# Values and six projection units of the second token half moved ahead of the attention loop

## The chip, the cores and the metric

The kernel runs on one core of a Trainium2 chip. The metric is the time of one execution on the device, in microseconds (us). Five engines matter here: PE (TensorE, matmuls), DVE (VectorE), ACT (ScalarE), POOL (GpSimd) and SP (SyncE), whose in-order queue issues nearly all DMA transfers.

## The reference

One layer of an encoder over 2048 tokens of 1024 features in float32, with 16 heads of 64:

```python
h = rmsnorm(x, norm_0)
q, k, v, gate = split(h @ w_in_0, 4)              # each 2048 x 1024
# tokens form a grid of 32 rows x 64 columns; a query sees 8 rows x 16 columns of keys
s = q . k / 8 + rpb[head, row offset, column offset]   # outside the window: -1e30
o = softmax(s) . v
x = x + (o * silu(gate)) @ w_out_0
out = rmsnorm(x, norm_f)
```

## The kernel before

All large matmuls are made of float32 values split in a high and a low part (`hi`, `lo`, or `h`, `l`): three products (hi.hi, hi.lo, lo.hi) replace one. A weight or input block is split by one ACT copy and one DVE or POOL subtraction.

The instruction order of every engine is written by hand (`manual_schedule`): each engine and the SP queue run their lists in program order, and wait by semaphores. `store(key, lag, f)` puts an action off until `lag` more filler matmuls have been issued.

Tokens are handled in four quarters `c` (0 to 3) of 512 tokens, and eight head pairs `p`. The kernel has two parts.

`stage_one` (L413) projects tokens 0 to 1023 (c = 0, 1): first the values (`values_of`, L468, matmul L475), then twelve units, one for each of `k`, `q`, `g` (gate) and four weight column groups `j`. A unit is computed with seven block products in place of eight (`product`, L508, matmul L517): 7 x 12 = 84 matmuls of 128x512, against 96 in the plain form. The price is sums of weight blocks on DVE (`sum_`, L502), sums of results (`add`, `out_`) and a scaling on POOL (L535). `give` (L341) splits q and k into high and low and stores them to DRAM (`q_hi`, `q_lo`, `k_hi`, `k_lo`).

Then a loop over 64 pieces (`pairs`; a piece is one head pair, one block `T` of 8 token rows, two of four column blocks `C`) does the attention. For each piece: `scores` (L819: 12 matmuls L832, then a fused add-and-minimum L839 on DVE and an exponential L842 on ACT), `normalise` (L845: reciprocal on DVE, scaling L850 on POOL), `turns` (L862: transposes L855 on PE, copies out of PSUM L879 on ACT and L880 on DVE) and `values` (L886, matmuls L900). Scores of piece i stand between the transposes and the values of piece i-1. Loads of a piece come from DRAM: `load_v` (L778, eight transfers `vt` of 36 to 64 KB for one piece, at L789), `load_qk` (L760, `kt` twice and `qt` twice for two pieces), `load_sg`, `load_e` (the bias table of a head pair, from which `bias`, L806, makes the masked tables `em`).

Between the pieces `feed` (L1114) issues filler matmuls: first `projections` (L715), the remaining plain projections of tokens 1024 to 2047 (c = 2, 3; `group` L365 with matmuls L374 to L378, `group_v` L384 with L393 to L397), then `outputs` (L1050), the output projection (L1087 to L1091). The list `amount` sets how many filler matmuls a piece gets, about 27 for most:

```python
amount = [44.0] * 2 + [(8 * 192 - 48 - 30 - 88) / 50] * 50 + [29.0] * 5 + [46.0] * 4 + [48.0] * (N + 1 - 61)
```

Pieces come in the order: block T = 0 of all head pairs, then T = 1, 2, 3 of head pair 0, of head pair 1, and so on. At most eight transfers of the SP queue are under way: each takes one of eight completion semaphores in turn, and waits for the transfer eight before it.

Of the kernel before, what the change touches and what calls it, by code (L numbers as in the profile page):

```python
# [25 lines left out]
EPS = 1e-6  # L26
# [44 lines left out]
def build(ctx, tc, x, xr, xt, wg, rpb, w_out, n0, nf, masks, out):  # L71
# [3 lines left out]
    q_hi = [dram.tile([128, S], F32, name=f"q_hi{p}") for p in range(NP)]  # L75
    q_lo = [dram.tile([128, S], F32, name=f"q_lo{p}") for p in range(NP)]
# [12 lines left out]
    wp = pool("wp", 10)  # L89
# [5 lines left out]
    xp = pool("xp", 4)  # L95
# [63 lines left out]
    def use_item(it):  # L159
# [3 lines left out]
        if kind == "x":  # L163
            split_x(a, b, t)
        elif kind == "w":
# [13 lines left out]
            (nc.gpsimd if (b + u) % 2 and state["half"] > 1 else nc.vector).tensor_tensor(l, t, h.bitcast(F32), OP.subtract)  # L179
# [8 lines left out]
    def square(t, half, tile_):  # L188
        c = t // 4
        if c not in rows:  # L190
            rows[c] = tiny.tile([128, 8], F32, name="ss")
        i = t % 4 if half is None else 2 * (t % 4) + half
        nc.scalar.activation(tile_, tile_, AF.Square, accum_out=rows[c][:, i:i + 1])

    def stats(c):
        ss = rows.pop(c)
        m = tiny.tile([128, 8], F32, name="m")[:, :4]
        if c < 2:
            nc.vector.tensor_tensor(m, ss[:, 0:8:2], ss[:, 1:8:2], OP.add)
            ss = m  # L200
        nc.vector.tensor_scalar(m, ss[:, :4], 1.0 / D, EPS, op0=OP.mult, op1=OP.add)
        rsqrt(rt[:, 4 * c:4 * c + 4], m, 4)
# [38 lines left out]
    for n, (k, j, ph, c) in enumerate(halves):  # L241
        a = (KINDS[k] + j, ph)
        wi = [("w", (u, ph), b) for b in range(4) for u in units(k, j)] if a not in seen else []
        xi = [("x", b, c) for b in range(NK)] if c not in seen else []
# [8 lines left out]
    def may_use(it):  # L253
        kind, a, b = it
        d = state["done_halves"]
        if kind == "w":
# [3 lines left out]
            return sum(1 + (KINDS["v"] <= t[0] < KINDS["g"]) for t in live | {tiles_(a, b)}) <= 10  # L260
# [80 lines left out]
    def give(kind, hp, c, tmp):  # L341
# [3 lines left out]
        if kind == "g":  # L345
# [38 lines left out]
    def group_v(w, t):  # L384
        c, o = divmod(t, 4)
        o = slice(o * 128, o * 128 + 128)
        p = bank(512, "pv")
        for k in range(NK):
            need(("x", k, c))
            for u in range(2):  # L390
                need(("w", (w[0] + u, w[1]), k // 2))
            h, l = wh[w, k // 2][:, k % 2], wl[w, k // 2][:, k % 2]
            nc.tensor.matmul(p, hh[k, c][:, o], h, start=(k == 0), stop=False)  # L393
            yield 1
            nc.tensor.matmul(p, hh[k, c][:, o], l, start=False, stop=False)  # L395
            yield 1
            nc.tensor.matmul(p, hl[k, c][:, o], h, start=False, stop=(k == NK - 1))  # L397
            if k % 2 and t % 4 == 3 and state["half"] == last_use["w", w]:
                freed.add((*w, k // 2))
            yield 1  # L400
            if k in (2, 5):
                consume(1)
        evac_v((w[0] - KINDS["v"]) // 2, t, p)

# [8 lines left out]
    def stage_one():  # L413
        us = [(k, j) for j in range(4) for k in "kqg"]
        order7 = (1, 6, 2, 7, 5, 4, 3)
        seq = [(n, P) for n in range(len(us)) for P in order7]
        uses = {1: ("A11", "B11"), 2: ("A12", "B21"), 3: ("S4", "B22"), 4: ("A22", "T4"),
                5: ("S1", "T1"), 6: ("S2", "T2"), 7: ("S3", "T3")}
        quarter = {"A11": 0, "A12": 1, "A21": 2, "A22": 3}
        A, F, B, U, W = {}, {}, {}, {}, {}  # L420
        X1 = {f: [(xs([128, 512], F32R, "h"), xs([128, 512], F32R, "l")) for _ in range(4)]
              for f in ("B12", "B11", "B21", "B22")}
        spot = mkp([128, 3, 512], F32, "spot")
        land = {f: [p([128, n], F32, "land")[:, :512] for _ in range(4)]
                for f, p, n in (("x12", kp, 960), ("x22", qp, 512), ("x11", vp, 512))}
        land["x21"] = [spot[:, k] for k in range(3)] + [lp([128, 512], F32, "land")]
        slots = [(mp, 512)] * 6 + [(vp, 512)] * 2 + [(sp, 512)] * 2 + [(pa, 768)] * 2 + [(vp, 512)] * 4
# [146 lines left out]
        for k in range(4):  # L574
            load_x("x12", k)
# [655 lines left out]
```

## Time and profile before

| | |
|---|---|
| median of 3 runs | 1109.18 us (1106.75 to 1109.65) |
| the profiled execution | 1107.81 us |
| its span, first to last instruction | 1105.7 us |
| mean granted TensorE clock | 0.995 |
| PE busy | 1086.1 us (98%) |
| DVE, ACT, POOL busy | 691.2, 512.7, 368.7 us |
| first score matmul, last value matmul | about 350 us, about 1032 us |
| moved by DMA | 228.32 MB, mean 206 GB/s |

A busy share is the time in which an engine had an instruction under way. Matmuls overlap in the pipeline, so the mean duration of one (about 390 ns for 128x512) is longer than the distance between two. The DMA share is the mean over the core's 16 DMA engines. "x" before a number counts instructions; an arrow `<-` in a wait names what the engine waited for.

### The profile page before, as it was taken

Reading aid. Unit: us, or ns where it says so; the run is one execution under the profiler, and the core shown is the slowest. Engines: PE = TensorE matmul, PEld = TensorE weight load, DVE = VectorE, ACT = ScalarE, POOL = GpSimd, SP = SyncE. Lnnn points to the kernel's source line nnn. Section 1 sums busy time; section 2 is a strip of 40 time slices with the busy share of each in tenths; the row PEclk is TensorE's granted clock in tenths of the full one; section 3 lists DMA queues with packets and bytes.
Section 4 is the critical chain, followed back from the end, with each engine's and each line's share of the span. In section 5 each row is a group of like instructions: output and inputs, shape, how many; then the busy total and the mean of one; then the engine's idle time right before and its main releaser. Section 6 shows DMA issues by size and latency. Waiting matters only on the chain. (4 is left out here: it accounts for less than half of the span.)

```text
span 1105.7 us, 22346 instructions
## 1 busy us (share of the span) xinstructions
PE 1086.1 (98%) x7693; PEld 887.0 (80%) x7693; DVE 691.2 (63%) x1621; ACT 512.7 (46%) x1286; POOL 368.7 (33%) x441
## 2 busy tenths in 40 slices
PE   9999999999989999999999999999999999999997
PEld 6888888888868788888888778887888888888885
DVE  5555889889877543465555555446466767566534
ACT  7734443434345544554445444455444555444322
POOL 0000313222222643445444444244542473342200
PEclk9999999999999999999999999999999999999999
DMA  9634645464489977788888678678787889765342
GB/s 314 218 78 118 199 149 198 157 195 128 133 252 272 292 235 222 214 252 239 250 236 229 215 209 255 175 206 252 209 236 222 272 253 252 224 207 154 119 143 76
DMA packets 147856, 228.32 MB, mean 206 GB/s; under 512 B 18592, under 2 KB 63648, under 8 KB 147744
## 3 DMA queue, kind: packets, MB, share of 16 engines
q1 hardware_dynamic: 147600, 226.63, 68.5%
q8 instruction: 62, 1.02, 0.4%
q14 instruction: 50, 0.41, 0.1%
q10 hardware_dynamic: 144, 0.26, 0.1%
HBM read 159.71 MB, written 67.11 MB: 205 GB/s over the span
## 5 line engine op out<-in xcount | busy, mean ns | idle before, releaser
L850 POOL TENSOR_SCALAR x<-x,st 128x360 f32<-128x360 f32 (+5 forms) x256 | 157.5, 634 | 226.0 <-DVE st L848 217.3
L842 ACT ACTIVATE x<-x,st 128x360 f32<-128x360 f32 (+5 forms) x256 | 151.8, 594 | 45.3 <-DVE st L839 45.3
L378 PE MATMUL pp<-hh,w 128*128 128x512 f32 x384 | 152.3, 397 | 1.1 <-DVE w L179 1.1
L374 PE MATMUL pp<-hh,w 128*128 128x512 f32 x384 | 151.0, 393 | 0.0
L376 PE MATMUL pp<-hl,w 128*128 128x512 f32 x384 | 150.3, 391 | 0.0
L535 POOL TENSOR_TENSOR tmp<-tmp,rb 128x512 f32<-128x512 f32 x36 | 58.9, 1635 | 272.9 <-DVE tmp L534 232.0
L880 DVE COPY pta<-ph 128x384 f32<-128x384 f32 (+3 forms) x128 | 61.6, 516 | 137.6 <-PE ph L855 137.2
L517 PE MATMUL pp<-h,f 128*128 128x512 f32 x384 | 125.4, 392 | 2.9 <-ACT hh L156 2.9
L839 DVE CUSTOM_DVE_ANT_0 x<-s,em 128x360 f32<-128x360 f32 (+5 forms) x256 | 123.8, 538 | 6.2 <-PE s L832 4.7
L879 ACT ACTIVATE pta<-ph 96x256 f32<-96x256 f32 (+1 forms) x224 | 59.8, 333 | 123.1 <-PE ph L855 122.8
L517 PE MATMUL pp<-t,f 128*128 128x512 f32 x432 | 104.2, 390 | 0.0
L900 PEld LDWEIGHTS o<-pta,vt 96*64 96x64 f32 (+2 forms) x1792 | 84.6, 138 | 16.5 <-issue 10.2
L1087 PE MATMUL po<-woh,gh 128*128 128x512 f32 x244 | 95.9, 393 | 0.0
L1091 PE MATMUL po<-wol,gh 128*128 128x512 f32 x244 | 95.4, 391 | 0.0
L517 PEld LDWEIGHTS pp<-t,f 128*128 128x128 f32 x432 | 80.9, 188 | 17.9 <-DVE u L528 1.2
L1089 PE MATMUL po<-woh,gl 128*128 128x512 f32 x244 | 95.2, 390 | 0.0
L900 PE MATMUL o<-pta,vt 128*64 128x128 f32 (+4 forms) x1792 | 93.4, 256 | 0.6 <-DVE pta L880 0.6
L832 PE MATMUL s<-kt,qt 64*128 64x360 f32 (+5 forms) x768 | 92.5, 353 | 0.4 <-DVE pta L880 0.4
L517 PEld LDWEIGHTS pp<-h,f 128*128 128x128 f32 x384 | 72.7, 189 | 18.5 <-ACT hh L156 3.3
L378 PEld LDWEIGHTS pp<-hh,w 128*128 128x128 f32 x384 | 72.1, 188 | 17.6 <-DVE w L179 1.5
L376 PEld LDWEIGHTS pp<-hl,w 128*128 128x128 f32 x384 | 72.1, 188 | 15.1
L374 PEld LDWEIGHTS pp<-hh,w 128*128 128x128 f32 x384 | 72.1, 188 | 14.8
(139 smaller groups left out, 1973.5 us busy)
## 6 DMA issues: line engine op xcount, KB each, us to landing
raw<-in_wg_dram SPq DMA_DIRECT2D x126, 256.0 KB
vt<-vd SPq DMA_DIRECT2D x256, 48.0 KB
e<-in_rpb_dram SPq DMA_DIRECT2D x36, 240.0 KB
vd<-v SPq DMA_DIRECT2D x32, 256.0 KB
k_hi<-hi SPq DMA_DIRECT2D x32, 256.0 KB
k_lo<-lo SPq DMA_DIRECT2D x32, 256.0 KB
q_hi<-hi SPq DMA_DIRECT2D x32, 256.0 KB
q_lo<-lo SPq DMA_DIRECT2D x32, 256.0 KB
```

The source lines that it names most:

```text
L374: nc.tensor.matmul(p, wh[w, b][:, cols], hh[k, c], start=(k == 0), stop=False)
L376: nc.tensor.matmul(p, wh[w, b][:, cols], hl[k, c], start=False, stop=False)
L378: nc.tensor.matmul(p, wl[w, b][:, cols], hh[k, c], start=False, stop=(k == NK - 1))
L517: nc.tensor.matmul(B[n, P], t[:, int(m == 2), c], x[k][int(m == 1)], start=P in (1, 6, 5) and k == 0 and m == 0, stop=k == 3 and m == 2, s ...
L832: nc.tensor.matmul(pst[s], qq[a, qs], kk[a, :r1 - r0, c0:c1], start=(m == 0), stop=(m == 2))
L839: nc.vector.tensor_tensor_reduce(X[i, C][s], pst[s], EM[p, ROW_TYPE[T], COL_TYPE[C], s], -1.0, 1e38, OP.add, OP.min, st[:, s:s + 1])
L842: nc.scalar.activation(X[i, C][s], X[i, C][s], AF.Exp, bias=st[:, s:s + 1], scale=-1.0, accum_out=st[:, 2 + s:3 + s])
L850: nc.gpsimd.tensor_scalar(X[i, C][s], X[i, C][s], st[:, 4 + s:5 + s], 0.5, op0=OP.mult, op1=OP.mult)
L900: nc.tensor.matmul(o[s * 64:s * 64 + 64, C * 128 + q0:C * 128 + q0 + nq], vt[C][:k, g - g0_, s * 64:s * 64 + 64], t[:k, at:at + nq], start ...
L1087: nc.tensor.matmul(p, gh, woh[q, j], start=(i == 0), stop=False)
L1089: nc.tensor.matmul(p, gl, woh[q, j], start=False, stop=False)
L1091: nc.tensor.matmul(p, gh, wol[q, j], start=False, stop=(i == NK - 1))
```

## The change

The values of tokens 1024 to 2047, and the units k, q, g of column groups j = 0 and 1 for these tokens, leave the filler of the attention loop. A new `stage_two` between `stage_one` and the loop computes them: the values with `values_of`, the six units with the seven products (`seven_products` is the old loop of stage one made into a function). The last unit of stage one loads and splits the first inputs and weights of stage two, the last unit of stage two those of the attention loop. The plain projections that stay as filler are the units of j = 2, 3 (`halves`): 576 matmuls in place of 1152 and 384 for values.

q is stored once, unsplit (`qd`), loaded once for two pieces and split on ACT and DVE by `split_q` after the second piece before its use. The transposes and values of a piece now run two pieces behind its scores, in place of one (`xp` has 8 buffers); the loads of `vt` move back by one piece as well. The pieces come by row group: T = 0 of all head pairs, T = 1 and 2 of all head pairs, T = 3 of all head pairs. Filler is 16 matmuls for each of the first 48 iterations and 20 for each of the last 18.

```diff
-    q_hi = [dram.tile([128, S], F32, name=f"q_hi{p}") for p in range(NP)]
-    q_lo = [dram.tile([128, S], F32, name=f"q_lo{p}") for p in range(NP)]
+    qd = [dram.tile([128, S], F32, name=f"qd{p}") for p in range(NP)]
...
-    wp = pool("wp", 10)
+    wp = pool("wp", 8)
...
-    xp = pool("xp", 4)
+    xp = pool("xp", 8)
...
-    halves = []
-    for j in range(4):
-        us = [(k, j) for k in "kqvg" if k != "v" or j % 2 == 0]
-        groups = [us[:2], us[2:3], us[3:]] if j == 0 else ([us[:1], us[1:]] if j == 3 else [[u] for u in us])
-        for g in groups:
-            for c in (2, 3):
-                halves += [(k, j, 1, c) for k, j in g]
+    units_two = [(k, j) for j in range(2) for k in "kqg"]
+    halves = [(k, j, 1, c) for j in range(2, 4) for g in (("k", "q", "g") if j == 2 else ("k", "qg")) for c in (2, 3) for k in g]
+    attending = [False]
...
+        written.add((kind, hp, c))
+        if kind == "q":
+            store(("q", hp, c), 12, lambda: nc.sync.dma_start(qd[hp][:, s], tmp))
+            return
         hi = ev([128, 512], F32R, "hi")
         lo = ev([128, 512], F32R, "lo")
-        if kind == "q":
-            nc.scalar.activation(hi, tmp, AF.Copy, scale=HD ** -0.5)
-            nc.vector.scalar_tensor_tensor(lo, tmp, HD ** -0.5, hi.bitcast(F32), op0=OP.mult, op1=OP.subtract)
-        else:
-            nc.scalar.activation(hi, tmp, AF.Copy)
-            (nc.vector if c < 2 else nc.gpsimd).tensor_tensor(lo, tmp, hi.bitcast(F32), OP.subtract)
-        dh, dl = (q_hi, q_lo) if kind == "q" else (k_hi, k_lo)
-        written.add((kind, hp, c))
-        store((kind, hp, c), 12, lambda: (nc.sync.dma_start(dh[hp][:, s], hi.bitcast(F32)),
-                                          nc.sync.dma_start(dl[hp][:, s], lo.bitcast(F32))))
+        nc.scalar.activation(hi, tmp, AF.Copy)
+        (nc.gpsimd if attending[0] else nc.vector).tensor_tensor(lo, tmp, hi.bitcast(F32), OP.subtract)
+        store(("k", hp, c), 12, lambda: (nc.sync.dma_start(k_hi[hp][:, s], hi.bitcast(F32)),
+                                         nc.sync.dma_start(k_lo[hp][:, s], lo.bitcast(F32))))
...
-    def group_v(w, t):
...
+    def seven_products(us, c0, X1, also):
...
+        def run():
+            then = []
+            for i, (n, P) in enumerate(seq):
+                product(n, P)
+                kind, j = us[n]
...
+                ahead(i)
+                also(n - last, i - 7 * n)
+            for f in then:
+                f()
...
+    def values_of(X1, u, ts, ks):
+        for t in ts:
...
+            if n == 0:
+                if i == 0:
+                    for a, b in ((0, 0), (1, 0), (0, 1)):
+                        load_v0(0, a, b)
+                    X2["B11"] = [(xs([128, 512], F32R, "h"), xs([128, 512], F32R, "l")) for _ in range(4)]
+                    for k in (0, 1):
...
+        ahead, run = seven_products(us, 0, X1, also)
...
+    def stage_two():
+        x12, x11, x21 = L2["x12"], L2["x11"], L2["x21"]
+        x22 = [qp([128, 512], F32, "land") for _ in range(4)]
...
-                    load_e(0, xp)[1]()
-                if P != 1:
+                if i in (1, 2, 3, 4):
+                    consume(1)
+                if i == 5:
                     consume(2)
-                if P in (5, 4):
-                    bias(0, 0, (5, 4).index(P))
-                if P == 4:
+                if i in (4, 5):
+                    bias(0, 0, i - 4)
+                if i == 3:
                     for f in load_qk(0, 0):
                         f()
-        for f in then:
-            f()
+                if i == 5:
+                    split_q(0, 0)
+
+        ahead, run = seven_products(units_two, 2, X2, also)
...
+        pair(0, (8, 9), w(0, 3), both(lw(1, 0), block("B12", x12, 0, 1)), block("B12", x12, 2, 3), block("B22", x22, 0, 1))
+        pair(0, (10, 11), both(v(0, 8, 9), block("B22", x22, 2, 3)), lambda: diagonal(2), t123(0), both(t123(1), lw(1, 1)))
+        spread_rstd(2)
+        pair(0, (12, 13), v(0, 10, 11), t123(2), t123(3), both(t4(0, 1, 2, 3), lw(1, 2)))
+        pair(0, (14, 15), both(v(0, 12, 13), w(1, 0)), both(w(1, 1), lw(1, 3)), w(1, 2), w(1, 3))
+        pair(1, (12,), v(0, 14, 15), form("T2", x11, 0), form("T2", x11, 1))
+        pair(1, (13,), both(v(1, 12), form("T2", x11, 2)), form("T2", x11, 3), lambda: diagonal(3))
+        spread_rstd(3)
+        pair(1, (14,), both(v(1, 13), form("T3", x22, 0)), form("T3", x22, 1))
+        pair(1, (15,), both(v(1, 14), lambda: ahead(-9, -1)), form("T3", x22, 2), form("T3", x22, 3))
+        pair(1, (8,), both(v(1, 15), lambda: ahead(-8, -1)), t1(0), t1(1), lambda: ahead(-7, -1))
+        pair(1, (9,), both(v(1, 8), t1(2)), t1(3), lambda: ahead(-6, -1), form("T4", x21, 0))
+        pair(1, (10,), both(v(1, 9), form("T4", x21, 1)), form("T4", x21, 2), form("T4", x21, 3))
+        pair(1, (11,), both(v(1, 10), lambda: ahead(-5)), lambda: ahead(-4), both(lambda: ahead(-3), lambda: ahead(-2)),
+             both(lambda: ahead(-1), v(1, 11)))
+        for k in range(4):
+            hh[k, 2], hl[k, 2] = X2["B11"][k]
+            hh[k, 3], hl[k, 3] = X2["B12"][k]
+            hh[4 + k, 2], hl[4 + k, 2] = X2["B21"][k]
+            hh[4 + k, 3], hl[4 + k, 3] = X2["B22"][k]
+        run()
...
-    order = [(p, 0) for p in range(NP)]
-    order += [(p, T) for p in range(6) for T in (1, 2, 3)]
-    order += [(6, 1), (7, 1), (7, 2), (6, 2), (6, 3), (7, 3)]
+    order = [(p, 0) for p in range(NP)] + [(p, T) for p in range(NP) for T in (1, 2)] + [(p, 3) for p in range(NP)]
...
-        def queries(src):
-            t = qp([128, 512], F32R, "qt")
-            QT[p, T].append(t)
-            nc.sync.dma_start(t.bitcast(F32), src[p][:, T * 512:T * 512 + 512])
-
-        return [lambda: keys(k_hi), lambda: keys(k_lo), lambda: queries(q_hi), lambda: queries(q_lo)]
+        def queries():
+            QT[p, T] = t = qp([128, 512], F32, "qr")
+            nc.sync.dma_start(t, qd[p][:, T * 512:T * 512 + 512])
+
+        return [lambda: keys(k_hi), queries, lambda: keys(k_lo)]
+
+    def split_q(p, T):
+        t = QT[p, T]
+        QT[p, T] = h, l = qp([128, 512], F32R, "qh"), qp([128, 512], F32R, "ql")
+        split_to(h, l, t, HD ** -0.5)
...
-            if T and p == lastp[T]:
+            if T == 3 and p == lastp[T]:
...
-    amount = [44.0] * 2 + [(8 * 192 - 48 - 30 - 88) / 50] * 50 + [29.0] * 5 + [46.0] * 4 + [48.0] * (N + 1 - 61)
+    early = 96 * (12 - len(units_two)) + 192
+    amount = [early / 48] * 48 + [(384 - 24) / 18] * 18
...
     def prepare(i):
-        p, T, cs = pairs[i]
-        m = i // 2
-        nx = order[m + 1] if m + 1 < len(order) else None
-        ty = ROW_TYPE[T]
         all_loads()
-        fs = load_v(p, T, cs[0]) + load_v(p, T, cs[1])
-        if cs[0] == 0:
-            for key in [key for key in EM if key[:2] != (p, ty)]:
-                del EM[key]
-            later_loads(fs, 0, 2)
-            if nx:
-                later_loads(load_qk(*nx), 3, 4)
-        else:
-            if nx and nx[0] != p:
-                later_loads(load_e(nx[0]), 0, 1)
-            later_loads(fs, 2, 2)
-            later_loads([lambda: load_sg(p, T)], 18, 0)
+        if 0 < i <= N:
+            p, T, cs = pairs[i - 1]
+            later_loads(load_v(p, T, cs[0]) + load_v(p, T, cs[1]), 0, 1)
+            if cs[0] == 2:
+                later_loads([lambda p=p, T=T: load_sg(p, T)], 9, 0)
+        if i < N:
+            p, T, cs = pairs[i]
+            nx = order[i // 2 + 1] if i // 2 + 1 < len(order) else None
+            if cs[0] == 0:
+                for key in [key for key in EM if key[:2] != (p, ROW_TYPE[T])]:
+                    del EM[key]
+                if nx:
+                    later_loads(load_qk(*nx), 10, 2)
 
     def tables(i):
         p, T, cs = pairs[i]
@@ -1161,32 +1292,34 @@
         ty = ROW_TYPE[T]
         if cs[0] == 0:
             bias(p, ty, 2) if (p, ty, 2, 0) not in EM else None
-        elif nx and (nx[0], ROW_TYPE[nx[1]]) != (p, ty):
-            EM.clear()
-            for cty in (0, 1):
-                bias(nx[0], ROW_TYPE[nx[1]], cty)
+            if nx and nx[0] != p:
+                later_loads(load_e(nx[0]), 5, 1)
+        elif nx:
+            split_q(*nx)
+            if (nx[0], ROW_TYPE[nx[1]]) != (p, ty):
+                EM.clear()
+                for cty in (0, 1):
+                    bias(nx[0], ROW_TYPE[nx[1]], cty)
 
     stage_one()
-    feed(14)
-    bias(0, 0, 2)
-    feed(16)
-    for i in range(N + 1):
+    stage_two()
+    attending[0] = True
+    for i in range(N + 2):
         a = amount[i]
         feed(a * 0.45)
-        if i:
+        prepare(i)
+        feed(a * 0.55, 8)
+        if 0 < i <= N:
             normalise(i - 1)
-        if i < N:
-            prepare(i)
-        feed(a * 0.55, 8)
-        if i:
-            turns(i - 1)
-        if i == N:
+        if i > 1:
+            turns(i - 2)
+        if i == N + 1:
             all_loads()
             feed(6)
         if i < N:
             scores(i)
-        if i:
-            values(i - 1)
+        if i > 1:
+            values(i - 2)
         if i < N:
             tables(i)
     while next(outs, 0) != 0:
```

More of the change, by code (lines that the diff above doesn't have):

```diff
@@ L243, in build @@
         wi = [("w", (u, ph), b) for b in range(4) for u in units(k, j)] if a not in seen else []
-        xi = [("x", b, c) for b in range(NK)] if c not in seen else []
+        xi = [("x", b, c) for b in range(4)] if c == 3 and c not in seen else []
         seen |= {a, c}
@@ new lines, in t4, with g, form @@
+        def t4(*ks):
+            def g():
+                for k in ks:
+                    d = x21[k]
+                    nc.vector.scalar_tensor_tensor(d, d, gain("x21", k), x11[k], op0=OP.mult, op1=OP.subtract)
+            return g
+        def form(f, x, *ks):
+            def g():
+                for k in ks:
+                    h, l = (p([128, n], F32R, "t")[:, :512] for p, n in slots[f][2 * k:2 * k + 2])
+                    X2.setdefault(f, []).append((h, l))
+                    split_to(h, l, x[k], None)
+            return g
```

453 lines of the change are left out of this document (256 added, 197 removed).

## The prediction

> **What bounds the kernel now.** I read the page's busy times first, then the windows by stage.
>
> ```profile
> span 1105.7 us, 22346 instructions
> PE 1086.1 (98%) x7693; PEld 887.0 (80%) x7693; DVE 691.2 (63%) x1621; ACT 512.7 (46%) x1286; POOL 368.7 (33%) x441
> ...
> DMA  9634645464489977788888678678787889765342
> ```
>
> PE is the bound: 98% of the span. The DMA row steps up from about 0.5 to about 0.8 where the attention begins (a third of the way). The windows say the same in numbers; columns are busy us of PE, PEld, DVE, ACT, POOL with counts, then granted clock, DMA share, GB/s.
>
> ```profile
> 100.00:150.00 50.00, 50.00 (x222) 41.42 (x221) 42.01 (x57) 19.55 (x35) 11.15 (x7) 1.00 0.58 178
> 200.00:250.00 50.00, 50.00 (x222) 41.42 (x221) 42.82 (x56) 20.19 (x36) 13.26 (x9) 1.00 0.51 163
> 300.00:350.00 50.00, 45.99 (x197) 37.07 (x195) 39.51 (x49) 20.37 (x34) 15.86 (x11) 0.97 0.81 249
> 350.00:400.00 50.00, 48.25 (x374) 39.34 (x375) 30.34 (x89) 27.43 (x77) 25.92 (x33) 0.97 0.87 265
> 345.00:425.00 80.00, 78.05 (x624) 63.56 (x624) 43.59 (x128) 40.02 (x114) 34.55 (x47) 0.98 0.85 265
> 950.00:1000.00 50.00, 50.00 (x367) 41.02 (x367) 31.36 (x91) 22.36 (x61) 22.64 (x26) 1.00 0.65 197
> ```
>
> From 100 to 150 us only 128x512 matmuls run, 222 of them in 50 us: one costs 50 / 222 = 0.225 us of PE. PE loses time only at the passage into the attention (4.0 us in 300:350, 1.75 in 350:400).
>
> **The matmuls removed.** The instruction lists of the two built kernels hold 3725 and 3653 matmuls of 128x512; all other PE work has equal counts. Six units of 84 in place of 96 make the 72: 72 x 0.225 = 16.2 us, all on the bound. The profiled execution took 1107.8 us (span 1105.7 and 2.1 around it), 0.1% under the median of 1109.2. With nothing else changed: 1107.8 - 16.2 = 1091.6 us.
>
> **Stage two itself.** Its 384 value matmuls and 504 product matmuls are the forms of stage one, where PE stays at 50.00 of 50 with DVE at 42 to 43. A unit has the same DVE work, less the splits of q. I price it at 0; PE covers it, as long as DVE stays under about 43 of 50. The passage into the attention (some 9 us with the clock at 0.97, in rows 300:350 and 350:400) is now prepared in the last unit, and a second passage, between the stages, is new: 0, with -6 to +6 as bounds.
>
> **The attention loop, PE's share.** 888 x 0.225 = 200 us of PE work leave the loop, while its transposes, scores and loads stay. So a piece becomes shorter, and everything that goes with it must be done in less time. The timeline (start, duration, engine, line, form, count) gives PE's own attention work in one piece, from the first transpose to the next filler matmul, for T = 0, T = 1 or 2, T = 3:
>
> ```profile
> 451.01 0.74 PE L855 MATMUL ph<-ident,x 64*128 64x64 f32 x17
> 454.22 0.50 PE L397 MATMUL pv<-wh,hl 128*128 128x512 f32 x1
> ...
> 608.21 0.92 PE L855 MATMUL ph<-ident,x 64*128 64x64 f32 x24
> 611.74 0.50 PE L374 MATMUL pp<-hh,w 128*128 128x512 f32 x1
> ...
> 999.93 0.81 PE L855 MATMUL ph<-ident,x 64*128 64x64 f32 x18
> 1003.16 0.50 PE L1087 MATMUL po<-woh,gh 128*128 128x512 f32 x1
> ```
>
> That is 3.2, 3.5 and 3.2 us. With 16 fillers (3.6 us; 20 for T = 3, 4.5 us) and 0.1 us between filler and transposes, two pieces take PE 13.8, 14.5 and 15.6 us.
>
> **The attention loop, the SP queue.** This is the term that decides. From 345 to 425 us SP issued these transfers:
>
> ```profile
> DMA packets 14676, 21.19 MB, mean 265 GB/s; under 512 B 1962, under 2 KB 7802, under 8 KB 14667
> ...
> raw<-in_wg_dram SPq DMA_DIRECT2D x15, 256.0 KB
> e<-in_rpb_dram SPq DMA_DIRECT2D x8, 240.0 KB
> vt<-vd SPq DMA_DIRECT2D x32, 48.0 KB
> kt<-k_hi SPq DMA_DIRECT2D x4, 352.0 KB
> kt<-k_lo SPq DMA_DIRECT2D x4, 352.0 KB
> vt<-vd SPq DMA_DIRECT2D x32, 36.0 KB
> qt<-q_hi SPq DMA_DIRECT2D x4, 256.0 KB
> qt<-q_lo SPq DMA_DIRECT2D x4, 256.0 KB
> q_hi<-hi SPq DMA_DIRECT2D x4, 256.0 KB
> q_lo<-lo SPq DMA_DIRECT2D x4, 256.0 KB
> sgt<-sgd SPq DMA_DIRECT2D x4, 256.0 KB
> k_hi<-hi SPq DMA_DIRECT2D x3, 256.0 KB
> k_lo<-lo SPq DMA_DIRECT2D x3, 256.0 KB
> ogd<-og SPq DMA_DIRECT2D x3, 256.0 KB
> vd<-v SPq DMA_DIRECT2D x3, 256.0 KB
> raw<-in_xt_dram SPq DMA_DIRECT2D x1, 256.0 KB
> ```
>
> 128 transfers in 80 us: 1.6 per us, 265 GB/s. SP's waits in this stretch, and a run of five `vt` issues:
>
> ```profile
> SPq L789 <- DMA e<-in_rpb_dram: 5.1, 6, 2.2
> ...
> SPq L149 <- DVE st L839: 1.0, 4, 0.3
> ...
> 405.51 2.31 SPq L789 DMA_DIRECT2D vt<-vd  x5
> ```
>
> The longest wait is for an earlier transfer (5.1 us); the longest for an engine is 1.0 us in all. So over 80 us SP was never held up by data that was not there, and issued as fast as its own pace and its eight completion slots let it. I take this as near what the queue can do.
>
> What does the changed kernel ask of it? Its SP list, cut at every second piece, has on average 26.1 transfers and 3.6 MB for two pieces of T = 0 (8 such pairs), 25.75 and 4.0 MB for T = 1, 2 (16 pairs), about 27 and 4.1 MB for T = 3 (8 pairs); 16 of each are `vt`. At PE's pace this is 1.9, 1.8 and 1.7 transfers per us: more than was seen.
>
> - Lower bound, by bytes: at 265 GB/s the pairs take 13.6, 15.1 and 15.5 us, over PE's time only for T = 1, 2: 16 x 0.6 = 10 us. Below that, 0, if the stretch's pace was PE's and not the queue's: PE was busy 78.05 of its 80 us.
> - Upper bound, by count: at 1.6 per us they take 16.3, 16.1 and 16.9 us: 8 x 2.5 + 16 x 1.6 + 8 x 1.3 = 56 us.
> - My value prices the two kinds apart: a `vt` issue 2.31 / 5 = 0.46 us, so 64 of them 29.4 us and the other 64 transfers (80 - 29.4) / 64 = 0.79 us each. Pairs then take 16 x 0.46 + 10.1 x 0.79 = 15.3, 15.1 and 16.0 us: 8 x 1.5 + 16 x 0.6 + 8 x 0.4 = 25 us. It is nearest to the row, since it gives the row's own 80 us back.
>
> The merged q saves four 256 KB transfers of a group's eight for q and k, already in these counts. A late `vt` holds up the values (L900) at the head of PE's queue, with the fillers of the next piece behind them; a late `kt` holds up the scores.
>
> The Trainium skill, "DMA: Bandwidth & Descriptors", section "Bandwidth", speaks against the change: transfers under 64 KB are governed by their descriptors, not their bytes, and one of 64 KB is given 0.95 us; 16 `vt` end to end would by it be an estimated 15.2 us of every pair. The trace is milder, with 0.46 us for each, since several are under way at once.
>
> **DVE.** A fused score pass and a copy out of PSUM cost:
>
> ```profile
> L839 DVE CUSTOM_DVE_ANT_0 x<-s,em 128x360 f32<-128x360 f32 (+5 forms) x256 | 123.8, 538 | 6.2 <-PE s L832 4.7
> L880 DVE COPY pta<-ph 128x384 f32<-128x384 f32 (+3 forms) x128 | 61.6, 516 | 137.6 <-PE ph L855 137.2
> ```
>
> Four passes and two copies are 3.2 us of a piece of about 7.3; DVE also does gates, tables, half of q's split, and fillers' evacuations. In 950:1000, where fillers are output matmuls, DVE is busy 31.36 of 50 with 48 fillers in a piece of about 14 us; with 20 in 7.8 us I estimate 85 to 95%. The row 200:250 shows 86% beside an unhindered PE. Price 0, at most 0.5 us for each of the last 16 pieces: 8 us.
>
> **The transposes two pieces behind** cost no instruction. They give exponential and scaling two pieces. From 340 to 1010 us PE waited for that chain, and its weight loads for `vt`, only so long (us, times, longest):
>
> ```profile
> PE ph L855 <- POOL x L850: 4.4, 9, 1.2
> ...
> PEld o L900 <- DMA vt<-vd: 2.1, 6, 0.3
> ```
>
> The chain could give back 4.4 us at most; at the faster pace I take 0.
>
> **Sum.** 1107.8 - 16.2 + 25 + 0 + 0 = 1116.6, say 1117 us: slower by 0.8%. A difference of 0.3% (3.3 us) is about what can be told from none.
>
> **Rivals.**
>
> - *Everything fits: faster.* Price of the queue 0 to 10 us, so 1091.6 to 1102; I put it at 1094. For it: weight loads waited for `vt` 2.1 us in the whole loop, and q needs fewer transfers. Against it: 1.8 transfers per us were seen nowhere for 80 us. It decides if SP sustains 1.8 per us. The skill's section "Bandwidth" sets the limit of one core's HBM traffic at about 358 GB/s; by it alone 4.0 MB take an estimated 11 us of 14.5, and the result is 1091.6. The stretch's mean of 265 GB/s is below it and settles nothing. Chance 0.36.
> - *The count governs: much slower.* Eight slots and the issue time hold SP at 1.6 per us in all of the loop; 1091.6 + 56 = 1148. For it: the only row. Against it: its transfers are 165 KB on average, the new ones 140 to 155. Chance 0.12.
> - *A wash:* the queue gives back 13 to 20 us, 1105 to 1112. Chance 0.08.
> - That the matmuls are not removed is excluded by the instruction lists.
>
> My own case, a queue cost of 20 to 45 us with the other terms near 0, has 0.44. Faster is 0.36, same 0.08, slower 0.56. The range of 1090 to 1143 reaches over most of the first rival and into the second, and takes in the passages' 6 us and DVE's 8.
>
> **What would show it.** Right: windows of the loop with PE below 49 of 50, a DMA share of 0.9 or more, waits of `o` (L900's heir) for `vt` or of `s` for `kt` or `qr`, SP at about 1.65 transfers per us with no wait for engines; the two stages before at 50.00. Wrong: PE at 50.00 in the loop with SP at 1.75 or more (first rival), PE waits that name DVE's or ACT's `pta` copies, or lost time in stage two.

## The result, and the profile after

The changed kernel takes 1168.88 us (median of 4 runs, 1167.71 to 1174.97) against 1108.88 us for the kernel before on the same chip: the ratio is 1.0555, with a 95% interval of 1.0515 to 1.0596. It is slower, as forecast, but by 60 us and not by 8, and outside the range of 1090 to 1143. The profiled execution is the slowest of the four (1174.97 us), 6 us over the median; sums over its trace carry these 6 us.

The page of the changed kernel, its busy times, the granted clock in 40 slices, and the DMA totals:

```profile
span 1173.2 us, 22564 instructions
...
PE 1106.4 (94%) x7621; PEld 897.2 (76%) x7621; DVE 760.5 (65%) x1734; ACT 538.3 (46%) x1348; POOL 351.9 (30%) x430
...
PEclk9999999999999999999898999989898969998999
DMA  8634544444653353456777788778787685777442
...
DMA packets 142098, 215.80 MB, mean 184 GB/s; under 512 B 17952, under 2 KB 64544, under 8 KB 141984
```

PE's share fell from 98% to 94% although 72 matmuls are gone, and its clock has dents in the second half only. PE's busy time rose by 20 us (1086.1 to 1106.4) with less work, while the mean granted clock fell from 0.995 to 0.960: matmuls at a lower clock last longer. The windows (columns as in the prediction):

```profile
450.00:500.00 50.00, 50.00 (x222) 41.39 (x221) 39.96 (x53) 15.54 (x28) 14.30 (x9) 1.00 0.39 127
550.00:600.00 50.00, 43.55 (x399) 35.05 (x396) 27.93 (x88) 24.44 (x82) 26.66 (x39) 0.86 0.77 228
800.00:850.00 50.00, 42.88 (x390) 33.02 (x388) 32.47 (x76) 25.58 (x73) 19.27 (x25) 0.90 0.81 246
950.00:1000.00 50.00, 37.48 (x347) 30.37 (x348) 27.22 (x89) 22.05 (x67) 18.96 (x29) 0.80 0.69 207
533.00:1110.00 577.00, 521.33 (x5046) 417.25 (x5046) 364.15 (x1091) 298.24 (x900) 255.38 (x363) 0.92 0.73 219
```

and the loop of the kernel before as one window:

```profile
350.00:1031.00 681.00, 675.20 (x5884) 551.49 (x5886) 389.14 (x1117) 331.11 (x948) 294.73 (x387) 1.00 0.78 229
```

Stage two runs at 50.00 of 50. The loop is 104 us shorter, but 850 fewer fillers (1088 in place of 1938, counted from the first score to the last value matmul) should have shortened it by 850 x 0.225 = 191 us: it loses 87 us. Everything else cancels to 4 us in the kernel's favour: for the spans, 1105.7 - 16.2 + 87 - 4 = 1173.

Where the 87 us lie, summed piece by piece over the timeline (an undisturbed piece has 3.09 or 3.55 us of transposes, scores and values): 53 us in pieces that take longer than in the kernel before, in bursts of 1 to 9 us every few pieces; 17 us in one place at 940 us, where two pieces stand together with no filler between and take 24.3 us in place of 7.1; 17 us among the fillers, some 13 of them at half clock behind such bursts and 4 in a wait for an output's input at 845 us. One burst in the timeline of PE (start, duration, line, form, count, and in brackets the idle time before and its releaser):

```profile
564.47 0.39 PE L965 MATMUL s<-kt,ql 64*128 64x264 f32 x2
570.65 1.40 PE L965 MATMUL s<-kt,qh 64*128 64x352 f32 x4 [5.79 <-DVE tmp L326]
571.56 0.78 PE L965 MATMUL s<-kt,ql 64*128 64x352 f32 x2
572.27 2.40 PE L1033 MATMUL o<-pta,vt 96*64 96x128 f32 x24
574.60 0.80 PE L369 MATMUL pp<-h,w 128*128 128x512 f32 x1
575.20 0.63 PE L365 MATMUL pp<-h,w 128*128 128x512 f32 x1
575.62 0.63 PE L367 MATMUL pp<-l,w 128*128 128x512 f32 x1
```

PE's scores wait 5.79 us, for DVE's evacuation `tmp`. Behind the wait fillers start 0.42 us apart in place of 0.23: half clock. Why was `tmp` late? The waits of all engines from 563 to 578 us:

```profile
POOL em L947 <- DMA e<-in_rpb_dram: 9.3, 1, 9.3
...
PE s L965 <- DVE tmp L326: 5.8, 1, 5.8
DVE ql L499 <- ACT qh L498: 4.1, 1, 4.1
DVE em L947 <- DMA e<-in_rpb_dram: 3.4, 1, 3.4
ACT qh L498 <- DMA qr<-qd: 3.2, 1, 3.2
```

So the engine named is not the cause. DVE works in order; it stood at `ql` (whose `qr` had not landed) and then at `em` (whose bias tile `e` had not landed), with `tmp` behind both and PE's scores behind `tmp`. A late DMA shows here as a wait for DVE. Over the loop DVE waits 21.6 us for `e`, in 12 pieces (before: 5.6 us in 3), POOL 64.2 us (before: 25.7), and ACT 14.3 us for `qr`.

SP, 600 to 900 us, its longest waits and the transfers that are most of its list:

```profile
SPq L922 <- DMA kt<-k_lo: 20.8, 18, 2.0
SPq L922 <- DMA kt<-k_hi: 11.1, 12, 1.9
SPq L922 <- DMA qr<-qd: 10.3, 14, 1.5
SPq L922 <- DMA e<-in_rpb_dram: 8.5, 18, 1.1
...
SPq L1050 <- DVE og L1047: 3.0, 2, 1.7
```

```profile
kt<-k_hi SPq DMA_DIRECT2D x15, 480.0 KB
vt<-vd SPq DMA_DIRECT2D x142, 48.0 KB
kt<-k_lo SPq DMA_DIRECT2D x14, 480.0 KB
vt<-vd SPq DMA_DIRECT2D x104, 64.0 KB
...
vt<-vd SPq DMA_DIRECT2D x36, 36.0 KB
```

The whole list has 450 transfers in 300 us, 1.50 per us, 282 of them `vt`. In SP's own record of the 300 us, 198 are issuing, 23 the steps between, 72 waits for one of the eight completion slots, and 4 waits for data that an engine had not made. In these 300 us SP is never idle for want of work. In the last part of the loop, from 884 to 1110 us, it is: there it waits for what DVE and ACT have not yet made.

```profile
SPq L1050 <- DVE og L1047: 15.0, 4, 8.1
...
SPq L1094 <- ACT xr L1137: 7.3, 3, 3.7
```

So from 884 us on it is not shown that the queue alone sets the pace.

### The profile page after: what moved, and what is told of

Read it like the earlier page. It is cut to its first block, busy times and chain, and to the rows that moved or that the text cites. A ratio compares the mean times of both kernels' runs of the same rounds, so it can differ in the third digit from the quotient of the medians.

```text
span 1173.2 us, 22564 instructions
## 1 busy us (share of the span) xinstructions
PE 1106.4 (94%) x7621; PEld 897.2 (76%) x7621; DVE 760.5 (65%) x1734; ACT 538.3 (46%) x1348; POOL 351.9 (30%) x430
## 5 line engine op out<-in xcount | busy, mean ns | idle before, releaser
L421 PE MATMUL pp<-h,f 128*128 128x512 f32 x576 | 186.4, 389 | 0.0
L421 PE MATMUL pp<-t,f 128*128 128x512 f32 x648 | 155.8, 389 | 0.1
L965 PE MATMUL s<-kt,qh 64*128 64x480 f32 (+5 forms) x512 | 89.7, 384 | 29.9 <-DVE tmp L328 6.5
L1033 PE MATMUL o<-pta,vt 96*64 96x128 f32 (+4 forms) x1792 | 104.9, 275 | 9.7 <-ACT pta L1012 4.7
L421 PE MATMUL pp<-l,f 128*128 128x512 f32 x288 | 112.0, 389 | 0.0
L534 PE MATMUL pv<-wh,h 128*128 128x512 f32 x256 | 88.3, 390 | 0.9 <-ACT wh L516 0.9
L534 PE MATMUL pv<-wl,h 128*128 128x512 f32 x256 | 88.0, 390 | 0.3 <-DVE wl L517 0.3
L534 PE MATMUL pv<-wh,l 128*128 128x512 f32 x256 | 88.0, 389 | 0.0
L404 DVE TENSOR_TENSOR f<-raw,f 128x512 fp32r<-128x512 f32 x90 | 72.5, 806 | 22.7 <-ACT f L403 22.7
L947 POOL TENSOR_TENSOR em<-e,mk 128x264 f32<-128x264 f32 (+5 forms) x72 | 65.6, 922 | 68.4 <-DMA e<-in_rpb_dram 64.2
```

Source lines behind the costliest of these rows:

```text
L404: nc.vector.tensor_tensor(t[:, 1], src, t[:, 0].bitcast(F32), OP.subtract)
L421: nc.tensor.matmul(B[n, P], t[:, int(m == 2), c], x[k][int(m == 1)], start=P in (1, 6, 5) and k == 0 and m == 0, stop=k == 3 and m == 2, s ...
L534: nc.tensor.matmul(ps[t], a[:, o], b, start=k == 0 and m == 0, stop=k == NK - 1 and m == 2)
L965: nc.tensor.matmul(pst[s], qq[a, qs], kk[a, :r1 - r0, c0:c1], start=(m == 0), stop=(m == 2))
L1033: nc.tensor.matmul(o[s * 64:s * 64 + 64, C * 128 + q0:C * 128 + q0 + nq], vt[C][:k, g - g0_, s * 64:s * 64 + 64], t[:k, at:at + nq], start ...
```

## The experiments

Theory: SP's queue (issue time, and eight slots that a large transfer holds for long) sets the loop's pace. Rivals: the bytes; loads that are asked for too late in a queue that would do; the order two behind.

**1. Fewer, larger transfers.** v is stored by column blocks, so that a `vt` tile is one transfer:

```diff
-            nc.sync.dma_start(VT[p, T, C][r * w:r * w + w, :g1_ - g0_].rearrange("p g d -> p (g d)"), src[r])
...
-        return [lambda r=r: rows(r) for r in range(4)]
...
+            nc.sync.dma_start(VT[p, T, C][:4 * w, :g1_ - g0_].rearrange("p g d -> p (g d)"), src)
...
+        return [rows]
```

> The changed kernel with v stored by column blocks, so that a `vt` tile comes in one transfer of four times the bytes: 128 `vt` transfers in the loop in place of 512, the bytes the same; the stages get eight small stores of v for each value tile in place of one. Queue theory (SP's issue time and its eight completion slots set the loop's pace): 384 transfers less in a loop that issued 1.5 per us; the pairs of pieces fall from 26 transfers to 14, SP has room, PE's stalls of attention (53 us in excess of undisturbed pieces) and the stretches at half clock behind them (17 us) go for the most part: 1095 to 1120 us. Bytes theory (about 215 to 230 GB/s is what the DMA engines give with this mix): no change, 1160 to 1175. Lead theory (k and q of the next group are asked for one piece before they are used, however short the queue is): 20 us or less gained, 1150 to 1170.

Measured 1133.60 us (ratio to before 1.0231, 1.0192 to 1.027): 35 us faster than the changed kernel, above the 1120 us of the queue theory and below the 1150 of both others. A window of stage one, the loop, and SP's longest waits from 600 to 900 us:

```profile
50.00:100.00 50.00, 40.47 (x169) 32.69 (x168) 26.15 (x47) 20.82 (x36) 0.00 (x0) 0.90 0.58 125
543.00:1067.00 524.00, 494.89 (x5040) 399.17 (x5040) 359.11 (x1090) 297.26 (x900) 251.51 (x363) 0.97 0.80 240
```

```profile
SPq L1055 <- DVE og L1052: 78.8, 19, 8.4
SPq L1099 <- ACT xr L1142: 15.8, 5, 6.3
```

The loop is 53 us shorter with the same bytes, at 240 GB/s in place of 219; SP now waits for engines. The bytes theory falls: the DMA engines could give more. The lead theory allowed 20 us. Of the 53 us (6 of them peculiar to the execution that was profiled) some are given back in stage one: SP issues 48 small stores of v in 23 us, and a weight queued behind them stops PE for 9.5 us.

**2. More transfers in the kernel before.** Each `vt` transfer in two halves:

```diff
-            nc.sync.dma_start(VT[p, T, C][r * w:r * w + w, :g1_ - g0_].rearrange("p g d -> p (g d)"), src[r])
+            for a, b in ((0, 2), (2, g1_ - g0_)):
+                nc.sync.dma_start(VT[p, T, C][r * w:r * w + w, a:b].rearrange("p g d -> p (g d)"), src[r][:, a * 128:b * 128])
```

> The kernel before with each `vt` transfer in two halves: 1024 in the loop in place of 512, the bytes the same. Queue theory: the kernel before issued 1.45 transfers per us in its loop and could do little more than 1.6; 512 more at 0.4 us or so of issue are about 200 us of SP time, of which it had some 150 to 200 in slack: stalls as in the changed kernel, 1125 to 1200 us. Bytes theory: the same bytes, below 1115. Lead theory: nothing moves, 1109.

Measured 1222.00 us (ratio 1.1022, 1.1005 to 1.1038). With its bytes, order and matmuls unchanged, the kernel before becomes slower than the changed one, and than the 1200 us expected at most. (The loop of the kernel before had 1.39 transfers per us, not 1.45.) Waits, 350 to 1145 us:

```profile
POOL em L815 <- DMA e<-in_rpb_dram: 121.5, 16, 15.6
DVE em L815 <- DMA e<-in_rpb_dram: 86.5, 16, 11.1
...
PE o L901 <- DMA vt<-vd: 18.9, 14, 3.7
```

It is the changed kernel's picture, enlarged. SP issued 564 transfers from 600 to 900 us, 1.88 per us at 191 GB/s, with 242 us of issuing and only 27 of waits for slots. The packets are not what holds it: the halves make more of them, but the DMA engines take 157 per us in this loop, against 151 in the kernel before and 140 in the changed one, and are busy for 0.67 of the 300 us, less than in both. So the pace is not one number: small transfers run at SP's issue time, a mix with 480 KB ones at 1.5 per us, held by the slots too.

**3. Longer pieces.** Three units in stage two in place of six:

```diff
-    units_two = [(k, j) for j in range(2) for k in "kqg"]
+    units_two = [(k, j) for j in range(1) for k in "kqg"]
...
```

> The changed kernel with three seven-product units in the second stage in place of six: 36 matmuls of 128x512 more in all (8.1 us of PE), and 22 fillers in a piece of T = 0, 1, 2 in place of 16, so a pair of pieces takes PE about 16.5 us in place of 13.8 to 14.5. Queue theory, and bytes theory as well (both say that the loop wants a time for each piece that PE's work fell below): faster than the changed kernel in spite of more work, 1110 to 1140 us. If PE's work set the time: 8 us slower, 1177. Lead theory: the lead in us grows with the piece, so somewhat faster too, 1140 to 1165.

Measured 1138.59 us (ratio 1.0272, 1.0254 to 1.0289): 36 matmuls more, and 30 us faster. By its list the loop holds 288 fillers more, 65 us of PE, and is only 12 us longer (589 against 577 us). PE's work was not what the loop waited for. Queue and bytes theory both expected this.

**4. k and q asked for earlier.**

```diff
-                    later_loads(load_qk(*nx), 10, 2)
+                    later_loads(load_qk(*nx), 1, 3)
```

> The changed kernel with the loads of k and q of the next group spread from the second filler after their preparation, every third one, in place of from the eleventh, every second: they enter SP's queue about 2 us earlier and less bunched, the number and the bytes the same. Lead theory: the waits of scores for k and q go, 1110 to 1140 us. Queue and bytes theories: the queue is as full as before and something else is late, 1155 to 1180.

Measured 1159.04 us (ratio 1.0454, 1.0433 to 1.0474): 10 us gained, where the lead theory asked for 30 or more. POOL still waits 56.7 us for `e`.

**5. Fillers kept for the hole at 940 us.**

```diff
-    amount = [early / 48] * 48 + [(384 - 24) / 18] * 18
+    amount = [(early - 40) / 48] * 48 + [(384 - 24 + 40) / 18] * 18
```

> The changed kernel with 40 filler matmuls moved from the first 48 pieces (16.0 to 15.2 each) to the last 18 (20.0 to 22.2). In all four traces of the changed kernel and its variants two pieces near 905 to 940 us stand together without any filler, 22 to 24 us in place of 7.1, and the first output matmul behind them waits 9 to 10 us for ACT's split of an `ograw` that was loaded just before. Theory of a hole (the outputs of T = 0 are used up before the last group of T = 1 is stored, so there is nothing to fill with): the hole and its half clock go, 15 to 20 us, of which the slower last pieces give back at most 9: 1148 to 1162 us. If the hole is only the queue's lateness: the wait moves, 1163 to 1175.

Measured 1170.68 us (ratio 1.0544, 1.05 to 1.0588): no gain. The two pieces stand apart now. In the trace the loop is 4.6 us shorter although it holds 31 fillers more (7 us of PE), so the hole did cost it some 12 us; but with fewer output matmuls left behind the loop, PE waits 3.5 us for the input of the next ones there and goes on at half clock. The profiled spans differ by 5.6 us, which is no more than the runs of one kernel do here.

**6 and 7. A second queue.** Every second `vt` transfer from ACT's queue, then from POOL's:

```diff
-            nc.sync.dma_start(VT[p, T, C][r * w:r * w + w, :g1_ - g0_].rearrange("p g d -> p (g d)"), src[r])
+            (nc.scalar if r % 2 else nc.sync).dma_start(VT[p, T, C][r * w:r * w + w, :g1_ - g0_].rearrange("p g d -> p (g d)"), src[r])
```

> The changed kernel with every second `vt` transfer issued from ACT's queue in place of SP's: 256 each, sizes and bytes the same. Theory that one queue's issuing and its slots set the pace: SP's transfers in the loop fall by a third, 1115 to 1145 us. Theory that the DMA engines' service of so many transfers sets it, whichever queue they come from: 1155 to 1180. Were the eight slots shared by both queues: in between, 1145 to 1165. ACT pays some 0.45 us for each, 115 us in 540 of which it is busy about 300.

Measured 1189.62 us (ratio 1.0737, 1.072 to 1.0754): slower, and above all three ranges. From 600 to 900 us SP issued 301 and ACT 136, together 1.46 per us, the old pace. In the records ACT's issues wait for the same semaphores as SP's, and ACT, in order, holds up the copies behind them. Its waits in the loop:

```profile
ACT pta L1012 <- DMA vt<-vd: 57.9, 17, 6.0
```

> The changed kernel with every second `vt` transfer issued from POOL's queue in place of SP's. From ACT's queue the total pace stayed at 1.46 per us and ACT's transfers waited for the same slots as SP's. If POOL's transfers have slots of their own, SP keeps 14 to 15 transfers and their slots for a pair of pieces, and the slots were the limit: 1110 to 1145 us, with POOL (25 busy of 50) paying some 0.5 us for each. If the DMA engines' service sets the pace: 1155 to 1180. If POOL becomes late with the scaling of `x` and the tables, waits of `ph` for `x` appear and it is over 1165.

Measured 1142.05 us (ratio 1.0293, 1.0273 to 1.0312): 27 us faster than the changed kernel. POOL's issues wait for semaphores of their own. SP 325 and POOL 147 issues in the 300 us make 1.57 per us, and PE is nearer to its own pace:

```profile
533.00:1076.00 543.00, 501.99 (x5034) 403.29 (x5032) 372.36 (x1089) 297.40 (x900) 386.08 (x619) 0.96 0.79 232
```

The Trainium skill, "DMA: Bandwidth & Descriptors", section "Issuing engines are not separate DMA queues", says that starting transfers from several engines saves only the time that the sequencer needs to start them. Both runs took about the same issuing off SP; one lost 21 us and one gained 27. What differs is the slots, whom the issuing engine holds up, and the kind of queue: the profile's page of the second run lists POOL's share as `software_dynamic`, 8192 packets for 12.87 MB, where ACT's share took 10752 for 12.86 MB. The three are not separated here.

**8. One behind again.** Transposes and values of piece i-1 behind the scores of piece i:

```diff
-        if i > 1:
-            turns(i - 2)
...
+        if i:
+            turns(i - 1)
...
```

> The changed kernel with the transposes and values one piece behind the scores, as in the kernel before (`vt` is asked for in the piece's own iteration, normalisation ahead of the second half of the fillers). Queue theory: the number of transfers is the same, so 1150 to 1180 us; the hole near 905 us gets one piece shorter, up to 7 us less. If the order two behind is the cause: back to PE's own time, 1095 to 1120. If two behind is what holds the loop up at all: over 1185, with waits of `ph` for `x`.

Measured 1216.02 us (ratio 1.0967, 1.0918 to 1.1015). PE's waits in the loop:

```profile
PE ph L988 <- POOL x L983: 67.9, 113, 4.2
```

In the short pieces exponential and scaling do not end within one. The order two behind is no cause of the loss; against the order one behind it saves 47 us.

**9 and 10. All remedies together, and without two of them.** Column blocks, their stores from POOL's queue, 40 fillers kept, k and q earlier:

```diff
-                    nc.sync.dma_start(dst, v[r * 64 + c0:r * 64 + c1].rearrange("p (h d) -> p h d", h=4))
+                    nc.gpsimd.dma_start(dst, v[r * 64 + c0:r * 64 + c1].rearrange("p (h d) -> p h d", h=4))
```

> Three edits together on the changed kernel: v by column blocks with one `vt` transfer each (1133 us alone), the 64 or so more stores of v in the stages issued by POOL's queue in place of SP's (SP spent 23 us on 48 of them in a row at 37 us, and PE then waited 9.5 us for a weight behind them and ran 10 us at half clock), 40 fillers kept for the two empty pieces near 905 us, and k and q asked for earlier. Sum from 1133: 14 for the start, 15 for the hole, 0 to 5 for the earlier loads: 1098 to 1108 us, just below the kernel before. If PE's attention stalls are the queue's alone and the hole is a queue effect, 1112 to 1120.

Measured 1108.26 us (10 runs; ratio 1.0000, 0.999 to 1.0011): level with the kernel before. (The blocks make 256 stores of v in place of 32, so 224 more, where 64 were expected.)

```profile
532.00:1046.00 514.00, 496.95 (x5085) 401.98 (x5085) 361.96 (x1100) 299.07 (x905) 255.98 (x364) 0.99 0.81 245
```

> The changed kernel with column blocks for v and POOL's queue for the blocks' stores, without the 40 kept fillers and with k and q asked for as in the changed kernel: what lies between 1133.6 us (blocks alone) and 1108.3 (all together). The start's loss goes: 1117 to 1121 us. If the hole near 905 us is real where the queue has room, it stands in this trace (two pieces without a filler between, 22 us or so) and is worth the 10 to 15 us to the combined version; if not, this is at 1108 to 1112 already.

Measured 1121.85 us (ratio 1.0116, 1.0097 to 1.0135). The hole stands in it, with PE 8.87 us idle for ACT's `gh`. Keeping fillers and the earlier loads are worth 13.6 us together here, where SP has room; which of the two brings it was not tried. Alone, on the changed kernel, keeping fillers brought nothing and the earlier loads 10 us.

**11 and 12. Two searches for a faster version.** The combined version with three units (the edit of experiment 3), and the kernel before with column blocks and POOL's stores:

> The combined version (column blocks for v, POOL's queue for their stores, 40 fillers kept for the empty pieces, earlier k and q; 1108 us) with three units in the second stage in place of six: 36 matmuls of 128x512 more, 8.1 us of PE. What is left of its stalls is 26.5 us of attention in excess of undisturbed pieces and 5.7 of fillers at half clock, against 14.1 and 1.7 in the kernel before; with 22 fillers a piece the excess should come down to the kernel before's, 16 us at most. Queue and handover theory: 1100 to 1108 us. If the rest is not of the pieces' length: 1116.

Measured 1110.39 us (ratio 1.0012, 1.0001 to 1.0024), above what was expected. The attention's excess did come down, from 26.5 to 16.3 us, but the 8.1 us of matmuls ate it.

> The kernel before with v by column blocks, one `vt` transfer for each, and POOL's queue for the blocks' stores: 384 transfers less in its loop, bytes the same. The kernel before had PE 98% busy, 14 us of attention in excess of undisturbed pieces and hardly a half clock; its queue had room. Queue theory: little to gain, 1098 to 1109 us. If the column blocks bring a gain of their own, whatever the queue's load (the 35 us that they brought the changed kernel): 1075 to 1090.

Measured 1114.07 us (ratio 1.006, 1.0038 to 1.0083), 5 us above the range expected. Column blocks gain nothing where the queue has room. PE's wait for POOL's `x` rose from 4.4 to 8.0 us; the likely reason, not tested alone, is POOL's issuing inside the loop. No version beat the kernel before.

**13 and 14. The place of `e` in the queue.** Same transfers, but `e` asked for one piece earlier for DVE and five fillers earlier for POOL, in a ring of three buffers; then with the edit of experiment 4:

```diff
+            t = (pool_ or (ep if ring[0] % 3 else lp))([128, 512], F32, "e")[:, :480]
...
+        if i < N and i % 2 == 0 and i // 2 + 1 < len(order) and order[i // 2 + 1][0] != pairs[i][0]:
+            load_e(order[i // 2 + 1][0])[1]()
...
-                later_loads(load_e(nx[0]), 5, 1)
+                load_e(nx[0])[0]()
```

> The changed kernel with the next bias tile `e` of DVE asked for one piece earlier (ahead of the eight `vt` of its iteration, in a third buffer) and that of POOL five fillers earlier; number, sizes and bytes of the transfers the same. In the changed kernel DVE waits 21.6 us in 12 pieces for `e`, with `tmp` and `pta` queued behind it and PE's scores behind those; this is nearly each of the bursts. Theory of order (the queue would do, if `e` were not asked for last): DVE's waits for `e` go, PE's bursts with them, 1105 to 1135 us. Theory of pace (SP's queue as a whole is too slow for pieces of this length, and `e` is only the transfer on which that shows): the bursts move to other names (`qr`, `kt`, `vt`), 1150 to 1170.

Measured 1165.10 us (ratio 1.0509, 1.0453 to 1.0566; not to be told from the changed kernel). Waits in the loop:

```profile
POOL em L950 <- DMA e<-in_rpb_dram: 28.5, 9, 8.3
ACT qh L498 <- DMA qr<-qd: 27.9, 14, 4.7
...
DVE og L1050 <- DMA sgt<-sgd: 8.6, 5, 3.1
...
PE s L968 <- DMA kt<-k_lo: 6.0, 8, 1.7
```

> The same with k and q of the next group asked for earlier too (which alone gave 10 us). Theory of order: everything is asked for early, 1095 to 1125 us. Theory of pace: SP's 1.5 transfers per us remain and the loop takes what they take, 1145 to 1165.

Measured 1150.90 us (ratio 1.0378, 1.0345 to 1.0411). DVE's waits for `e` are gone in both. In the first, `qr` (27.9 us, before this edit 14.3), `kt` and `sgt` are late in its place; in the second `sgt` (32.4 us, against 3.7 in the changed kernel), while POOL still waits 51.3 us for its `e`. SP issues 1.51 and 1.57 per us. The two edits of order are worth 18 us together; the rest they do not touch, as the theory of pace expected. Other orders were not tried.

## Why the prediction was wrong

- **Removed matmuls, stage two, passages:** right. 72 matmuls are gone, stage two is at 50.00, and outside the loop 4 us were gained (bounds -6 to +6).
- **The SP queue, +25 us:** the mechanism was right and the size wrong; 87 us were lost in the profiled execution. The step that failed is the price of a `vt` transfer, 0.46 us. It was read from one run of five that found their slots free, and all waiting for slots in that stretch went to the other 64 transfers (0.79 us each). But other runs of `vt` in the same stretch wait too, here 0.78 and 0.62 us for each:

```profile
385.19 4.69 SPq L789 DMA_DIRECT2D vt<-vd  x6
...
420.51 4.32 SPq L789 DMA_DIRECT2D vt<-vd  x7
```

  From the end of one issue in SP's record to the end of the next, a `vt` took 0.61 us in the stretch and another transfer 0.65; in the changed kernel, from 600 to 900 us, 0.70 and 0.62. At 0.70 and 0.62 the prediction's pairs take 17.5, 17.2 and 18.0 us, so 8 x 3.7 + 16 x 2.7 + 8 x 2.4 = 92 us in place of 25. Since a pair has 16 `vt` among 26 transfers and the stretch had half, the cheap price for `vt` made 1.7 transfers per us out of a queue that gave 1.50. The rival "the count governs" thus had the mechanism, and its pace of 1.6 was still 6% too fast (56 us).

  The agreement of 92 with 87 is no independent check: the prices are read from the loop that they explain. Nor is 1.50 a fixed rate. SP issued 1.59 per us from 584 to 684 us, 1.45 over the whole loop, and 1.57 with the same transfers in the order of experiment 14. What shows the mechanism are the runs that change the transfers: 35 us less with fewer of them, 113 more with more.
- **What a late transfer stops:** named were `vt` for the values and `kt` for the scores. In the changed kernel's loop no matmul waits for `vt` (weight loads 0.8 us), and the scores wait 0.7 us for `kt`; late are `e`, `qr` and once `sgt` (3.7 us), and they stop POOL, DVE and ACT first. "DVE: price 0" counted its work, not its waiting in order.
- **The clock:** left out. Behind waits the granted clock fell to one half, 96 us in all in the changed kernel (14 before), which cost some 13 us in the fillers alone. These are part of the 87 us, not beside them, and where SP sets the pace a full clock would only have made PE wait longer; how much of them is the clock's own is open.
- **The hole:** left out. The changed kernel uses up the outputs of T = 0 before those of T = 1 can be loaded, and now sends the last group of T = 1 and 2 through DRAM. It is 17 us of the trace. Without it (experiment 5) the loop did some 12 us better for its work, and the time as a whole was the same; whether the hole is the queue's or its own is open.
- **Two behind, 0:** right in that it cost nothing; but the 4.4 us that it might give back were read in long pieces, and in short ones it is worth 47.
- **What would show it:** stages at 50.00, and loop windows under 49 of 50 (all but one, 49.32): seen. No waits of SP for engines: seen until 884 us, not after. A DMA share of 0.9 and 1.65 transfers per us: not seen, 0.73 and 1.50. Waits of `o` for `vt` or of `s` for `kt` or `qr`: not seen but for the 0.7 us. A sign of "wrong", PE waits that name `pta` copies, did show (14.5 us), with `qr` and `e` late behind ACT and DVE in the burst shown above. The estimate for DVE of 85 to 95% in the last pieces was too high as well: even in the faster version of experiment 9 it is 69.19 of 100 us, from 946 to 1046.
- **Why all remedies only level it:** with column blocks and their stores on POOL's queue (experiment 10) 47 of the 77 us between the changed kernel and PE's own 1091.6 are gone, and 13.6 more with kept fillers and earlier loads. The combined version still has 12 us more of attention excess (26.5 against 14.1) and 4 us more of half clock in fillers (5.7 against 1.7) than the kernel before, as much as the 16.2 us of matmuls that it saves. PE's waits there name `pta` and `gh`, that is ACT's and DVE's handovers. That more DVE or ACT time would free them was not tried, so the cause of these last 17 us is open.

## What to carry to other kernels

Count what a loop asks of its queue per unit of time, at the pace that the queue has shown with the same mix of sizes; when work is moved out of a loop, everything that stays must fit in the shorter time, and a few per cent in that pace decide the sign. Price a kind of transfer from all of its issues, waits for slots included, and not from one run of them that did not wait. When PE's wait names an engine that works in order, look what that engine itself waits for: a late transfer often stands one or two engines behind the name. Test a suspected queue by changing the number of transfers with the bytes kept, in both directions; here it moved the two kernels by -35 and +113 us.

## What the runs showed of the hardware

- One SP queue gave 1.50 transfers per us at 223 GB/s with a mix of 36 to 512 KB, and 1.88 per us at 191 GB/s with `vt` of 12 to 32 KB; with `vt` in single transfers of 144 to 256 KB (experiment 1) the core moved 249 GB/s at 0.88 per us, and SP waited for engines.
- ACT's transfers waited for the same eight completion semaphores as SP's, POOL's for eight of their own (experiments 6 and 7).
- Short waits cost clock. Here PE is idle for 1.81 and 0.60 us, and what follows is at half clock:

```profile
770.29 0.49 PE L965 MATMUL s<-kt,qh 64*128 64x480 f32 x1 [1.81 <-DVE tmp L328]
771.38 0.76 PE L965 MATMUL s<-kt,qh 64*128 64x480 f32 x3 [0.60 <-ACT pta L1012]
771.72 0.83 PE L965 MATMUL s<-kt,ql 64*128 64x480 f32 x2
772.48 2.83 PE L1033 MATMUL o<-pta,vt 96*64 96x128 f32 x32
```

The clock records show half clock for 6.8 us from 771.9. The Trainium skill, "TensorE: Matmul & The Clock Gate", section "Why this matters for your kernels", advises to avoid idle gaps of more than about 3 us; in this loop, with small matmuls around the waits, single waits of 1.8 to 2.8 us were enough, nine times; one of 1.15 us at 996 us was not.
